# Batch norm over 64 tiles: the stores of the first 61 tiles move from ScalarE's hardware queue to GpSimd's software queue

## The chip, the cores and the metric

The kernel runs on one core of one Trainium2 chip. The metric is the device time of one execution in microseconds (us); lower is better. The profiles come from the hardware profiler, one execution each.

## The reference

Batch normalisation with given statistics, in float32, on an input of 32 x 256 x 128 x 128. Mean, variance, gamma and beta have one value per channel (256 of them).

```python
return gamma * (x - mean) / np.sqrt(var + eps) + beta
```

Per channel this is one multiplication and one addition per element. The input is 536.9 MB and so is the output.

## The kernel before

The input is seen as 64 tiles of 128 channels by 16384 values: 128 partitions with 64 KB each, 8.39 MB a tile. Three buffers in SBUF hold one tile each; tile i uses buffer i % 3 and is normalised in place. A short beginning loads the four parameter vectors and turns them into `scale_t` and `shift_t`, one column per half of the channels.

The order of the work is written out by hand, engine by engine, with semaphores (`loaded`, `stored` per buffer, `vdone` and `adone` for the two compute engines).

- **Loads** are issued by SyncE (SP). Tile 0 comes in two halves (L90, L97). Tiles 1 and 2 follow at once (L104). From tile 3 on, a load waits first until its buffer's store has landed (L103) and then until VectorE has done the first part of the tile before it. So one load is in flight at a time.
- **VectorE (DVE)** waits until a tile has landed and does its first 14336 columns in two instructions: columns 0 to 2560 (`STEP`), then 2560 to `VCOLS` (L132). The first of the two releases the next load.
- **ScalarE (ACT)** does the last 2048 columns (L143). In the loop it waits for both VectorE parts of the tile and for the landing of the store before, then computes, and then issues the tile's store (L156):

```python
for i in range(last):
    nc.scalar.wait_ge(vdone, 2 * (i + 1))
    inst = scalar_part(i, VCOLS)
    if i:
        inst._wait_ge(stored[(i - 1) % NBUF], 16 * ((i - 1) // NBUF + 1))
    store(i)
```

So one store is in flight at a time too, except at the end: the last tile is split at column 9216 (`VLAST`) between the two engines, ScalarE computes its share on landing, and the last store doesn't wait for the one before.

GpSimd (POOL) does nothing in the loop. At the end SP waits for the three `stored` semaphores (L174).

Of the kernel before, what the change touches and what calls it, by code (L numbers as in the profile page):

```python
# [6 lines left out]


NBUF = 3
PAD = 936  # L10


STEP = 2560
VCOLS = 14336
VLAST = 9216


@with_exitstack
def kernel(
    ctx: ExitStack,  # L20
    tc: tile.TileContext,
    x: bass.AP,
    gamma: bass.AP,
    beta: bass.AP,
    running_mean: bass.AP,
    running_var: bass.AP,
    out: bass.AP,
):
    nc = tc.nc
    eps = 1e-5  # L30
    f32 = mybir.dt.float32

    N, C, H, W = x.shape
    P = nc.NUM_PARTITIONS
    assert C % P == 0
    NCB = C // P
    HW = H * W
    NT = N * NCB
    B = 32
    NQ = P // B  # L40
    NE = 16
    NPAR = 4

    xr = x.rearrange("n (cb p) h w -> (n cb) p (h w)", p=P)
    outr = out.rearrange("n (cb p) h w -> (n cb) p (h w)", p=P)

    params = ctx.enter_context(tc.tile_pool(name="params", bufs=1))
    data = ctx.enter_context(tc.tile_pool(name="data", bufs=1))
    params.tile([P, PAD], f32, name="pad", tag="pad")
    bufs = [data.tile([P, HW], f32, name=f"t{s}", tag=f"t{s}") for s in range(NBUF)]  # L50
    rows = params.tile([B, NPAR * C], f32, name="rows", tag="rows")
    turned = params.tile([B, NPAR * C], f32, name="turned", tag="turned")
    par = params.tile([P, NPAR, NCB], f32, name="par", tag="par")
    eps_t = params.tile([P, 1], f32, name="eps_t", tag="eps")
    std_t = params.tile([P, NCB], f32, name="std_t", tag="std")
    rstd_t = params.tile([P, NCB], f32, name="rstd_t", tag="rstd")
    scale_t = params.tile([P, NCB], f32, name="scale_t", tag="scale")
    ms_t = params.tile([P, NCB], f32, name="ms_t", tag="ms")
    shift_t = params.tile([P, NCB], f32, name="shift_t", tag="shift")

    loaded = [tc.alloc_semaphore(f"loaded{s}") for s in range(NBUF)]
    stored = [tc.alloc_semaphore(f"stored{s}") for s in range(NBUF)]
    early = tc.alloc_semaphore("early")
    vdone = tc.alloc_semaphore("vdone")
    adone = tc.alloc_semaphore("adone")
    fetched = tc.alloc_semaphore("fetched")
    vec = tc.alloc_semaphore("vec")
    act = tc.alloc_semaphore("act")  # L70

    with tc.tile_critical():  # L72
        count = [0]

        def step(inst, sem=None, value=None):

            if sem is not None:
                inst._wait_ge(sem, value)
            elif count[0]:
                inst._wait_ge(vec, count[0])  # L80
            inst.then_inc(vec, 1)
            count[0] += 1
            return count[0]

        left, right = slice(0, HW // 2), slice(HW // 2, HW)
        last = NT - 1

        nc.sync.dma_start(out=bufs[0][:, left], in_=xr[0][:, left]).then_inc(early, 16)  # L90
        zeroed = step(nc.vector.memset(rows[:], 0.0))  # L91
        for r, ap in enumerate((running_var, gamma, beta, running_mean)):
            inst = nc.sync.dma_start(out=rows[0:NE, r * C : (r + 1) * C], in_=ap.partition_broadcast(NE))  # L93
            if r == 0:
                inst._wait_ge(vec, zeroed)
            inst.then_inc(fetched, 16)
        nc.sync.dma_start(out=bufs[0][:, right], in_=xr[0][:, right]).then_inc(loaded[0], 16)  # L97
        for i in range(1, NT):
            s, turn = i % NBUF, i // NBUF


            if turn:
                nc.sync.wait_ge(stored[s], 16 * turn)  # L103
            inst = nc.sync.dma_start(out=bufs[s][:], in_=xr[i]).then_inc(loaded[s], 16)  # L104
            if turn:
                inst._wait_ge(vdone, 2 * (i - 1) + 1)


        step(nc.vector.memset(eps_t[:], eps))  # L109
        step(nc.vector.transpose(out=turned[:], in_=rows[:]), fetched, 16 * NPAR)  # L110

        blocks = turned.rearrange("p (rc q b) -> p rc q b", q=NQ, b=B)
        flat = par.rearrange("p r cb -> p (r cb)")
        for q in range(NQ):
            placed = step(nc.vector.tensor_copy(out=flat[q * B : (q + 1) * B], in_=blocks[:, :, q, 0]))  # L115
        var_t, gamma_t, beta_t, mean_t = (par[:, r] for r in range(NPAR))
        nc.scalar.activation(  # L117
            out=std_t[:],
            in_=var_t,
            func=mybir.ActivationFunctionType.Sqrt,  # L120
            bias=eps_t[:],
            scale=1.0,
        )._wait_ge(vec, placed).then_inc(act, 1)
        step(nc.vector.reciprocal(out=rstd_t[:], in_=std_t[:]), act, 1)  # L124
        step(nc.vector.tensor_mul(out=scale_t[:], in0=gamma_t, in1=rstd_t[:]))  # L125
        step(nc.vector.tensor_mul(out=ms_t[:], in0=mean_t, in1=scale_t[:]))  # L126
        ready = step(nc.vector.tensor_sub(out=shift_t[:], in0=beta_t, in1=ms_t[:]))  # L127
        nc.vector.wait_ge(vec, ready)

        def vector_part(i, first, end):  # L130
            t, cb = bufs[i % NBUF], i % NCB
            return nc.vector.tensor_scalar(  # L132
                out=t[:, first:end],
                in0=t[:, first:end],
                scalar1=scale_t[:, cb : cb + 1],
                scalar2=shift_t[:, cb : cb + 1],
                op0=mybir.AluOpType.mult,
                op1=mybir.AluOpType.add,
            ).then_inc(vdone, 1)

        def scalar_part(i, first):
            t, cb = bufs[i % NBUF], i % NCB
            return nc.scalar.activation(  # L143
                out=t[:, first:],
                in_=t[:, first:],
                func=mybir.ActivationFunctionType.Identity,
                bias=shift_t[:, cb : cb + 1],
                scale=scale_t[:, cb : cb + 1],
            ).then_inc(adone, 1)

        def landed(i):
            return loaded[i % NBUF], 16 * (i // NBUF + 1)

        def store(i):
            s = i % NBUF
            nc.scalar.dma_start(out=outr[i], in_=bufs[s][:])._wait_ge(adone, i + 1).then_inc(stored[s], 16)  # L156

        vector_part(0, 0, HW // 2)._wait_ge(early, 16)
        vector_part(0, HW // 2, VCOLS)._wait_ge(*landed(0))
        for i in range(1, NT):  # L160
            vector_part(i, 0, STEP)._wait_ge(*landed(i))
            vector_part(i, STEP, VLAST if i == last else VCOLS)
        for i in range(last):
            nc.scalar.wait_ge(vdone, 2 * (i + 1))
            inst = scalar_part(i, VCOLS)
            if i:
                inst._wait_ge(stored[(i - 1) % NBUF], 16 * ((i - 1) // NBUF + 1))
            store(i)
        scalar_part(last, VLAST)._wait_ge(*landed(last))
        nc.scalar.wait_ge(vdone, 2 * NT)  # L170
        store(last)

        for s in range(NBUF):
            nc.sync.wait_ge(stored[s], 16 * ((NT - s + NBUF - 1) // NBUF))  # L174


# [28 lines left out]
```

## Time and profile before

| | |
|---|---|
| median of 3 runs | 2483.6 us (2483.05 to 2484.41) |
| span of the profiled execution | 2481.0 us |
| what lies around the span, by the runs' median | 2.6 us |
| busy: DVE, ACT, POOL | 508.8, 139.8, 0.2 us |
| DMA | 1073.85 MB, mean 433 GB/s over the span |
| issue to landing, median: load of a tile, store of a tile | 37.0 us, 36.5 us |

The span goes from the first to the last instruction that the profiler recorded. The profiled execution has no separate time of its own: its span is set against the runs' median. The DMA share is the mean busy share of the core's 16 DMA engines. Queue q1 carries SyncE's loads and q10 ScalarE's stores; a packet of either is a partition's row of 64 KB. Issuing a DMA is not counted as an engine's busy time.

### The profile page before, as it was taken

To read this page: it belongs to the slowest core of one execution; us is meant where nothing else is said; L and a number is where in the kernel's file an instruction comes from. 1 tells how busy PE (TensorE), PEld (TensorE's weight loads), DVE (VectorE), ACT (ScalarE), POOL (GpSimd) and SP (SyncE) were. 2 spreads that over 40 slices of the span, in tenths; PEclk is the share of its full clock that TensorE was granted. 3 is DMA by queue.
4 is the path that set the end of the run, shared out by engine and by line. 5 is a ranking of instruction groups with operands and counts; after the bars stand their busy time and mean duration, and the time that the engine had idled before them with its cause. 6 is when DMAs were issued, how large, how long until landed. Compare 5 with 4: busy or idle time off the path is not lost.

```text
span 2481.0 us, 516 instructions
## 1 busy us (share of the span) xinstructions
DVE 508.8 (21%) x139; ACT 139.8 (6%) x66; POOL 0.2 (0%) x4
## 2 busy tenths in 40 slices
DVE  2122121221212212122121221212212122121120
ACT  0000000000000000000000000000000000000001
POOL 0000000000000000000000000000000000000000
DMA  9999999999999999999999999999999999999999
GB/s 411 435 440 428 433 440 432 430 440 432 430 440 437 427 438 436 428 437 436 432 433 438 430 434 437 432 432 437 434 431 436 437 428 437 437 428 435 437 432 402
DMA packets 18708, 1073.85 MB, mean 433 GB/s; under 512 B 2128, under 2 KB 2192, under 8 KB 2192
## 3 DMA queue, kind: packets, MB, share of 16 engines
q1 hardware_dynamic: 9488, 536.94, 50.0%
q10 hardware_dynamic: 9216, 536.88, 49.9%
q14 instruction: 4, 0.03, 0.0%
HBM read 536.94 MB, written 536.87 MB: 433 GB/s over the span
## 4 chain that ended last, share of the span: by engine, by line
DMA 92%; DVE 4%; another core or an unknown queue 2%; ACT 0%; issue 0%; SPq 0%; DVEq 0%
DMA t<-in_x_dram 92%; DVE t L132 4%; ACT t L143 0%; SPq L93 0%; DVE rows L91 0%; DVE eps_t L109 0%; DVEq L200 0%; SPq L72 0%
## 5 line engine op out<-in xcount | busy, mean ns | idle before, releaser
L132 DVE TENSOR_SCALAR t<-t,scale_t,shift_t 128x11776 f32<-128x11776 f32 (+2 forms) x128 | 505.3, 3989 | 1928.8 <-DMA t<-in_x_dram 1928.7
L143 ACT ACTIVATE t<-t,shift_t,scale_t 128x2048 f32<-128x2048 f32 x64 | 138.2, 2159 | 2297.8 <-DMA out_dram<-t 2274.9
L110 DVE STREAM_TRANSPOSE turned<-rows 32x1024 f32<-32x1024 f32 x1 | 1.2, 1232 | 11.8 <-DMA rows<-in_running_mean_dram 11.8
L117 ACT ACT_TABLE_LOAD x1 | 1.3, 1283 | 0.9 <-SPq L72 0.9
L91 DVE MEMSET rows<- 32x1024 f32 x1 | 0.9, 912 | 1.2 <-SPq L72 1.2
L117 ACT ACTIVATE std_t<-par,eps_t 128x2 f32<-128x2 f32 x1 | 0.3, 295 | 14.0 <-DVE par L115 14.0
L115 DVE COPY par<-turned 32x8 f32<-32x8 f32 x4 | 0.6, 162 | 0.1
L124 DVE RECIPROCAL rstd_t<-std_t 128x2 f32<-128x2 f32 x1 | 0.2, 166 | 0.4 <-ACT std_t L117 0.4
L125 DVE TENSOR_TENSOR scale_t<-par,rstd_t 128x2 f32<-128x2 f32 x1 | 0.2, 162 | 0.0
L127 DVE TENSOR_TENSOR shift_t<-par,ms_t 128x2 f32<-128x2 f32 x1 | 0.2, 162 | 0.0
L126 DVE TENSOR_TENSOR ms_t<-par,scale_t 128x2 f32<-128x2 f32 x1 | 0.2, 160 | 0.0
L189 POOL MEMSET const-bfloat16-1.0<- 128x1 bf16 x1 | 0.1, 101 | 0.0
L189 POOL MEMSET const-uint8-127<- 128x1 uint8 x1 | 0.1, 101 | 0.0
L189 POOL MEMSET const-float32-0.0<- 128x1 f32 x1 | 0.1, 98 | 0.2 <-issue 0.2
L189 POOL MEMSET const-float32-1.0<- 128x1 f32 x1 | 0.1, 98 | 0.0
L109 DVE MEMSET eps_t<- 128x1 f32 x1 | 0.1, 59 | 0.1
## 6 DMA issues: line engine op xcount, KB each, us to landing
t<-in_x_dram SPq DMA_DIRECT2D x2, 4096.0 KB, 15.9
out_dram<-t ACTq DMA_DIRECT2D x64, 36.5
t<-in_x_dram SPq DMA_DIRECT2D x63, 37.0
rows<-in_running_var_dram SPq DMA_DIRECT2D x1, 16.0 KB, 11.1
rows<-in_gamma_dram SPq DMA_DIRECT2D x1, 16.0 KB, 10.9
rows<-in_beta_dram SPq DMA_DIRECT2D x1, 16.0 KB, 10.7
rows<-in_running_mean_dram SPq DMA_DIRECT2D x1, 16.0 KB, 10.6
```

The costliest lines, as they stand in the source:

```text
L91: zeroed = step(nc.vector.memset(rows[:], 0.0))
L109: step(nc.vector.memset(eps_t[:], eps))
L110: step(nc.vector.transpose(out=turned[:], in_=rows[:]), fetched, 16 * NPAR)
L115: placed = step(nc.vector.tensor_copy(out=flat[q * B : (q + 1) * B], in_=blocks[:, :, q, 0]))
L117: nc.scalar.activation(out=std_t[:], in_=var_t, func=mybir.ActivationFunctionType.Sqrt, bias=eps_t[:], scale=1.0,)._wait_ge(vec, placed).t ...
L124: step(nc.vector.reciprocal(out=rstd_t[:], in_=std_t[:]), act, 1)
L125: step(nc.vector.tensor_mul(out=scale_t[:], in0=gamma_t, in1=rstd_t[:]))
L126: step(nc.vector.tensor_mul(out=ms_t[:], in0=mean_t, in1=scale_t[:]))
L127: ready = step(nc.vector.tensor_sub(out=shift_t[:], in0=beta_t, in1=ms_t[:]))
L132: return nc.vector.tensor_scalar(out=t[:, first:end], in0=t[:, first:end], scalar1=scale_t[:, cb : cb + 1], scalar2=shift_t[:, cb : cb + 1 ...
L143: return nc.scalar.activation(out=t[:, first:], in_=t[:, first:], func=mybir.ActivationFunctionType.Identity, bias=shift_t[:, cb : cb + 1] ...
L189: nc = _bacc.Bacc("TRN2", target_bir_lowering=False, num_devices=1)
```

## The change

The stores of tiles 0 to 60 are issued by GpSimd, on its software queue, with `single_packet=True`. Each waits for the landing of the store before, for both VectorE parts and for ScalarE's part of its tile. The last three stores (`NTAIL`) stay on ScalarE's hardware queue and count on semaphores of their own (`closed`); of them, those of tiles 61 and 62 wait for the landing of the store before. ScalarE now waits for a tile's landing alone before it computes, in all tiles. When the store of tile 60 has landed, GpSimd executes a DRAIN. SP waits for six semaphores at the end. Loads, VectorE's work, the buffers and the split of the columns are the same.

```diff
+NTAIL = 3
...
+    closed = [tc.alloc_semaphore(f"closed{s}") for s in range(NBUF)]
...
+        soft = NT - NTAIL
+
+        def written(i):
+            if i < soft:
+                return stored[i % NBUF], 16 * (i // NBUF + 1)
+            return closed[i % NBUF], 16
+
         def store(i):
             s = i % NBUF
-            nc.scalar.dma_start(out=outr[i], in_=bufs[s][:])._wait_ge(adone, i + 1).then_inc(stored[s], 16)
+            if i < soft:
+                if i:
+                    nc.gpsimd.wait_ge(*written(i - 1))
+                nc.gpsimd.wait_ge(vdone, 2 * (i + 1))
+                inst = nc.gpsimd.dma_start(out=outr[i], in_=bufs[s][:], single_packet=True)
+            else:
+                nc.scalar.wait_ge(vdone, 2 * (i + 1))
+                if i < last:
+                    nc.scalar.wait_ge(*written(i - 1))
+                inst = nc.scalar.dma_start(out=outr[i], in_=bufs[s][:])
+            inst._wait_ge(adone, i + 1).then_inc(written(i)[0], 16)
...
-        for i in range(last):
-            nc.scalar.wait_ge(vdone, 2 * (i + 1))
-            inst = scalar_part(i, VCOLS)
-            if i:
-                inst._wait_ge(stored[(i - 1) % NBUF], 16 * ((i - 1) // NBUF + 1))
-            store(i)
-        scalar_part(last, VLAST)._wait_ge(*landed(last))
-        nc.scalar.wait_ge(vdone, 2 * NT)
-        store(last)
+        nc.scalar.wait_ge(vec, ready)
+        for i in range(NT):
+            scalar_part(i, VLAST if i == last else VCOLS)._wait_ge(*landed(i))
+            store(i)
+
+        nc.gpsimd.wait_ge(*written(soft - 1))
+        nc.gpsimd.drain()
 
         for s in range(NBUF):
-            nc.sync.wait_ge(stored[s], 16 * ((NT - s + NBUF - 1) // NBUF))
+            nc.sync.wait_ge(stored[s], 16 * ((soft - s + NBUF - 1) // NBUF))
+            nc.sync.wait_ge(closed[s], 16)
```

## The prediction, made before the changed kernel ran

> **What bounds the kernel now.** I read the page first (busy shares, DMA queues), then the windows by stage, the chain of waits in order of time, the DMA view in short stretches, and the groups by shape.
>
> From the page, the span and who is busy; in the queue lines, packets, MB and share of the 16 engines' span:
>
> ```profile
> span 2481.0 us, 516 instructions
> ...
> DMA  9999999999999999999999999999999999999999
> ...
> q1 hardware_dynamic: 9488, 536.94, 50.0%
> q10 hardware_dynamic: 9216, 536.88, 49.9%
> ```
>
> q1 carries the loads, q10 the stores. Together they fill 99.9% of the DMA engines; DVE has 21%, ScalarE 6%. The windows (start:end, length, DVE, ACT and POOL busy, clock, DMA share, GB/s) say where the missing part is:
>
> ```profile
> 0.00:62.00 62.00, 17.95 (x15) 3.67 (x3) 0.20 (x4) 1.00 0.97 408
> 62.00:2418.00 2356.00, 485.57 (x123) 127.64 (x61) 0.00 (x0) 1.00 1.00 434
> 2418.00:2481.00 63.00, 5.27 (x2) 8.46 (x2) 0.00 (x0) 1.00 0.93 403
> ```
>
> Only the first and last stretch are short of 434 GB/s: 3% of 62 us and 7% of 63 us, about 6 us in all. The 62 tiles between run with no idle DMA time. Nothing that only moves compute can bring a gain there; what can change the time is the DMA going idle. The chain of one tile (start, length, what) shows how near that is:
>
> ```profile
> 978.96 36.96 DMA t<-in_x_dram
> 1015.92 0.03 issue
> 1015.95 1.62 DVE t L132
> 1017.57 0.02 issue
> 1017.59 36.98 DMA t<-in_x_dram
> ```
>
> Only one load is in flight at a time: a load lands, DVE does its first 2560 columns, and only then is the next load issued. For these 1.67 us, and the start-up after them, there is no load. The DMA view of 2.4 us stretches around this landing (1016.8, 1024.0 and 1026.4 us) shows what fills the hole (queue: packets, MB, share):
>
> ```profile
> DMA packets 16, 1.05 MB, mean 437 GB/s; under 512 B 0, under 2 KB 0, under 8 KB 0
> q10 hardware_dynamic: 16, 1.05, 100.8%
> ...
> q10 hardware_dynamic: 10, 0.66, 63.0%
> q1 hardware_dynamic: 6, 0.39, 37.8%
> ...
> q1 hardware_dynamic: 10, 0.66, 63.0%
> q10 hardware_dynamic: 6, 0.39, 37.8%
> ```
>
> In the hole every engine moves store packets only. When both queues have work, the shares swap each 2.4 us: 10 engines on a store and 6 on a load, then the reverse. So each engine takes one 64 KB packet from one queue, then one from the other. A 8.39 MB transfer is 128 such packets, 8 per engine; a period of 38.64 us (1017.59 less 978.96) is 16 turns of 2.414 us. This taking of turns is what spreads a store over 36.5 us, so that one is always there when a load lands.
>
> **The change, part by part.** The durations of compute come from the groups by shape:
>
> ```profile
> L132 DVE TENSOR_SCALAR t<-t,scale_t,shift_t 128x11776 f32<-128x11776 f32 x62 | 397.3, 6407 | 0.0
> L143 ACT ACTIVATE t<-t,shift_t,scale_t 128x2048 f32<-128x2048 f32 x63 | 131.8, 2092 | 2285.3 <-DMA out_dram<-t 2274.9 <-DVE t L132 10.5
> L132 DVE TENSOR_SCALAR t<-t,scale_t,shift_t 128x2560 f32<-128x2560 f32 x63 | 101.6, 1613 | 1927.1 <-DMA t<-in_x_dram 1927.1
> ```
>
> *ScalarE on landing.* Its 2.09 us run beside DVE's 1.61 + 6.41 = 8.02 us instead of after the previous store's landing. The store of a tile can be issued 8.02 us after the tile lands. Alone this would take 2.1 us out of the gap between two stores; loads fill that gap now, so it is worth nothing at the end.
>
> *61 issues move from ScalarE to GpSimd.* On GpSimd each store waits for the store before it, DVE and ScalarE; only the next store is queued behind. SP's queue keeps its instructions and waits. No row shows a store issued by GpSimd. The nearest rows are SP's first load (issued at 0.95 us, packets from about 2.0, so 1.0 us to the first packet) and, far off, 8.02 us if GpSimd had to wait for a whole DVE tile. I take 2 us, between a hardware start and DVE's work but nearer the start; the ends 1.0 and 8.0 stay for the range. The Trainium skill (DMA: Bandwidth & Descriptors, Specifications) gives about 1 us to the first byte on this path against 0.6, an estimate of 0.4 us more than hardware; no run here shows it, and by it the start would be 1.4 us. In the forecast the start lies beside a running load and costs nothing.
>
> *One packet per store.* The diff sets `single_packet=True`. If the engine's turn is a packet, as the swapping shares show, a store's turn becomes 8 x 2.414 = 19.3 us on every engine, with no load packet in between. The Trainium skill (DMA: Bandwidth & Descriptors, Queues, rings and completion order) says the same as a rule: an engine "drains a whole packet (≈9-17 descriptors typical, spec ceiling ≤64) from one row's ring before switching"; the trace agrees for single 64 KB packets (2.414 us a turn), and nothing in it has a longer one.
>
> Follow a tile that lands at T with no store in flight. At T+1.67 the next load is issued, at T+2.7 its packets begin. At T+8.0 the store is issued, at T+10 its packet is there; the load has finished 3 packets and is in the 4th, so the burst runs from about T+12.4 to T+31.7. Four load packets remain: 9.7 us, to T+41.4, and the load is seen to land near T+42. The store finished 10 us before, and the next cannot be issued before T+50. So when that load lands nothing is in flight, and the cycle repeats. The same follows from any start: a burst and its wait for one turn take about 22 us plus the start, while a load needs at least 38.6, so stores always run out of tiles.
>
> The DMA is then idle from the last load packet to the first packet of the next load: about 0.4 us until DVE sees the landing (my estimate: the span ends 1.8 us after the last store packet, final barrier included), 1.67 us for DVE's first part and the issue, 1.0 us to the first packet, and 0.8 us because the landing counts the last of 16 engines (their first packets spread over about that much). 3.87 us a tile. It occurs at the landings of tiles 2 to 60, 59 times: 228 us. Bounds: 2.7 us without wake-up and spread (159 us), 5.0 us with twice of both (295 us).
>
> *Last three stores on ScalarE's queue.* These take turns of 64 KB again; the tail is as before, a few us either way. *Semaphores and DRAIN.* The DRAIN sits behind store 60's landing, more than two tiles (80 us) before the end, with nothing behind it on GpSimd; SP waits for six semaphores instead of three after everything has landed. Zero; at the end of the program, uncovered, well under the 1.8 us that the tail has now.
>
> *Sum.* Span 2481.0 + 228 = 2709 us. The runs' median lies 2.6 us above the profiled span, so 2712 us.
>
> **The rivals.**
>
> *Stores still take turns by 64 KB (the flag does not lengthen a turn), and the phase holds.* The store's gap is then 2 us instead of 2.09 + 0.34 + about 0.7 = 3.1 us from landing to first packet. A change of less than a turn leaves the alternation as it is. For: the period stood still at 16 turns all through the run although the two gaps differ. Against: the flag is in the program. Time: 2484 us, 2480 to 2491 with a turn lost at the start or end.
>
> *Turns of 64 KB, but the phase slips.* Now a store lands 24.1 us after a load (1015.95 to 1040.06 in the timeline), 16 us away from either limit: the tile not yet computed, or the buffer not yet free for the next load. If GpSimd starts over about half a turn later than hardware did (beyond 4.3 us from landing), or over half a turn earlier (below 1.5), each period gains or loses a turn, and after about seven tiles both queues wait on the same event. Then 1 to 3 us a tile are idle: 59 x 1 to 59 x 3, 2540 to 2660 us. A slip that settles sooner costs only 5 to 15 us. The Trainium skill (SBUF — State Buffer, the "DVE blocks DMA" trap) says that GpSimd cannot write descriptors during DVE's two-port operations; stores released in DVE's 8 us would start that much later, the slip's condition. No run here shows such a wait.
>
> *Faster: fewer packets, less overhead.* 448 packet boundaries per engine fewer. Were each worth 12 ns, 5 us would go: 2478 us. Against: consecutive packets start 2.414 us apart whichever queue came before, 27.1 GB/s per engine, and no gap between records is seen. The stretches outside full rate hold only 6 us, which the change leaves alone.
>
> **How the numbers follow.** The burst 0.50 (its own range 2640 to 2780); turns kept and phase held 0.25, of which nearly all within 0.2% (5 us, about what a measurement of this kernel can tell from no change); phase slipped 0.19, all but a little of it slower; faster 0.06. Slower: 0.50 + 0.18 + 0.02 = 0.70; same 0.24; faster 0.06. The likeliest case gives 2712. The range must reach down to the held phase to leave out less than 2 in 10, and up to the burst's upper bound: 2480 to 2775.
>
> **What would show it.** Right: stores landing in about 22 us after issue instead of 36.5, loads in about 40; stretches of 2.4 us with no q1 packets for 19 us in a row; a DMA share near 0.91 in the middle windows; a period near 42.5 us. Wrong: two queues still swapping each 2.4 us and a period of 38.64 us (held phase), or that swapping with idle slices (slip). A GpSimd issue that waits for DVE's end would show in the timeline as a store starting just behind DVE's second part.

## The result, and the profile after

The changed kernel takes 2580.1 us (median of 5 runs, 2571.2 to 2582.3) against 2483.6 us before: ratio 1.0381, 95% interval 1.0367 to 1.0395. It is slower by 3.8%, in the forecast range and in the forecast direction, but by 96 us instead of 228. The profiled execution took 2575.6 us, with a span of 2573.8.

The page after; q0 is the software queue. Columns of the queue lines: packets, MB, share of 16 engines' span.

```profile
span 2573.8 us, 524 instructions
...
q1 hardware_dynamic: 9488, 536.94, 51.2%
q0 software_dynamic: 8784, 511.71, 45.9%
q10 hardware_dynamic: 432, 25.17, 2.3%
...
t<-in_x_dram SPq DMA_DIRECT2D x63, 38.9
out_dram<-t POOLq DMA_DIRECT2D x61, 37.1
```

Two things to see. A store still takes 37 us from issue to landing, so it still shares the engines with a load: there is no burst of 19 us. And the added time sits in the load's queue. The times of the packet records, added up and divided by the 16 engines, give 1317 us for q1 against 1241 before (+76) and 1239 us for the stores in both kernels. What the packets leave of the span grows from 1 to 18 us (+17). Together that is the 93 us that the span gained: partly idle engines, mostly load packets that take longer than 2.418 us. The shares on the page, times the span, say the same within their rounding.

The windows by stage put it into the middle of the run:

```profile
0.00:62.00 62.00, 16.50 (x15) 5.76 (x4) 0.87 (x5) 1.00 0.99 407
62.00:2510.00 2448.00, 483.04 (x123) 127.77 (x61) 31.98 (x60) 1.00 1.00 418
2510.00:2574.00 64.00, 9.27 (x3) 6.36 (x1) 0.00 (x0) 1.00 0.90 380
```

GpSimd's 0.53 us for each issue are counted as its busy time here, unlike the issues of SyncE and ScalarE. There are 418 GB/s where there were 434. A busy share of 1.00 hides it, because a longer packet counts as busy: here the GB/s column is the one to read. The chain of one tile:

```profile
977.70 39.43 DMA t<-in_x_dram
1017.13 0.03 issue
1017.16 1.62 DVE t L134
1018.78 0.02 issue
1018.80 36.50 DMA t<-in_x_dram
```

The steps between landing and next issue are the same as before. The loads of this stretch take 36.4 to 39.6 us instead of a steady 36.96 to 36.98. And the waits say on what a store waits (the first line is of the kernel before, the other two of the changed one):

```profile
ACT t L143 <- DMA out_dram<-t: 2274.9, 62, 43.4
...
POOL out_dram L170 <- DVE t L134: 1696.2, 43, 41.1
POOL out_dram L170 <- DMA out_dram<-t: 704.0, 18, 42.8
```

Of 61 stores, 43 wait for compute of their own tile, 18 for the store before. In the kernel before, all but the first and the last store were held by the one before. The stores have moved ahead in time against the loads, up to the limit that compute sets. Where a store's landing lies behind a load's is called the phase here. VectorE starts with a load's landing, and an instruction released by a store starts 0.03 us (ScalarE) or 0.5 us (GpSimd) after that store's landing, so the timelines show the phase. First two lines of the kernel before:

```profile
1015.95 7.94 DVE L132 TENSOR_SCALAR t<-t,scale_t,shift_t 128x2560 f32<-128x2560 f32 x2 [30.69 <-DMA t<-in_x_dram]
...
1040.06 2.09 ACT L143 ACTIVATE t<-t,shift_t,scale_t 128x2048 f32<-128x2048 f32 x1 [36.51 <-DMA out_dram<-t]
```

Then the first tiles of the changed kernel:

```profile
93.33 7.93 DVE L134 TENSOR_SCALAR t<-t,scale_t,shift_t 128x2560 f32<-128x2560 f32 x2 [28.37 <-DMA t<-in_x_dram]
...
108.47 0.53 POOL L170 DMA_DIRECT2D out_dram<-t  x1 [35.89 <-DMA out_dram<-t]
...
134.88 7.93 DVE L134 TENSOR_SCALAR t<-t,scale_t,shift_t 128x2560 f32<-128x2560 f32 x2 [33.61 <-DMA t<-in_x_dram]
145.58 0.53 POOL L170 DMA_DIRECT2D out_dram<-t  x1 [36.57 <-DMA out_dram<-t]
...
176.75 7.94 DVE L134 TENSOR_SCALAR t<-t,scale_t,shift_t 128x2560 f32<-128x2560 f32 x2 [33.94 <-DMA t<-in_x_dram]
185.27 0.53 POOL L170 DMA_DIRECT2D out_dram<-t  x1 [39.16 <-DVE t L134]
```

A store used to land 24.1 us after a load. By the landings on record this falls here to 14.6, 10.2 and 4.8 us within the first tiles; from tile 4 on most stores wait for VectorE, and the phase stays near 4.8 (most tiles) or 9.7.

The DMA view in stretches of 2.4 us around the landing at 1017.13 us shows the consequence (stretches from 1016.8, 1024.0, 1026.4, 1028.8, 1031.2 and 1033.6 us):

```profile
DMA packets 16, 0.98 MB, mean 410 GB/s; under 512 B 1, under 2 KB 1, under 8 KB 1
q0 software_dynamic: 16, 0.98, 94.5%
...
q1 hardware_dynamic: 16, 1.05, 101.1%
...
q1 hardware_dynamic: 16, 1.05, 142.9%
...
DMA packets 2, 0.13 MB, mean 55 GB/s; under 512 B 0, under 2 KB 0, under 8 KB 0
...
q0 software_dynamic: 15, 0.98, 94.5%
q1 hardware_dynamic: 1, 0.07, 6.3%
...
q1 hardware_dynamic: 15, 0.98, 94.4%
q0 software_dynamic: 1, 0.07, 6.3%
```

The store is at its last packets when the load lands. Then the load is alone for four packets (the store of the tile cannot be issued before 1025.68). The fourth of these packets, just before the store's packets begin, is long: 16 packets start that hold 142.9% of the stretch, and in the next stretch only two packets start. Afterwards the engines move in step, 15 on one queue and 1 on the other, where before they were 10 and 6. On average (tiles 4 to 61) the first packets of a load take 2.81 us, the fourth 3.17, and the others 2.42 to 2.47. So of the 93 us about 23 sit in the first packets, 45 in the fourth, 17 in idle engines and the rest in the other packets.

### The profile page after: what moved, and what is told of

It is laid out like the page before. It is cut to its first block, busy times and chain, and to the rows that moved or that the text cites. A ratio compares the mean times of both kernels' runs of the same rounds, so it can differ in the third digit from the quotient of the medians.

```text
span 2573.8 us, 524 instructions
## 1 busy us (share of the span) xinstructions
DVE 508.8 (20%) x139; ACT 139.9 (5%) x66; POOL 32.8 (1%) x65
## 4 chain that ended last, share of the span: by engine, by line
DMA 92%; DVE 4%; another core or an unknown queue 2%; ACT 0%; issue 0%; SPq 0%; DVEq 0%
DMA t<-in_x_dram 92%; DVE t L134 4%; ACT t L145 0%; SPq L95 0%; DVE rows L93 0%; DVE eps_t L111 0%; DVEq L219 0%; SPq L74 0%
## 5 line engine op out<-in xcount | busy, mean ns | idle before, releaser
L170 POOL DMA_DIRECT2D out_dram<-t x61 | 32.6, 535 | 2400.2 <-DVE t L134 1696.2
```

Source lines behind the costliest of these rows:

```text
L170: inst = nc.gpsimd.dma_start(out=outr[i], in_=bufs[s][:], single_packet=True)
```

## The experiments

Theory P (phase): what counts is the length of two gaps, the load's (landing to the first packet of the next load) and the store's (likewise). If they match, the taking of turns holds its phase; if the store's is shorter by half a turn or more, stores slip early up to the compute limit and the hole at the landing is no longer covered. Theory Q: the software queue itself makes load packets slow.

By the records the store's gap is 5.5 to 7.0 us in the kernel before, in the first tiles 6.0 to 6.4, against 6.1 to 6.4 for the load. In the first tiles of the changed kernel it is 4.2 to 4.5 us against 6.3. These are counted to the first of the 16 engines' packets. The expectations below give the store's gap up to half a us longer. Each ratio is against the kernel before.

### e1: the hardware queue, ScalarE on landing

```diff
-            if i < soft:
-                ...
-                inst = nc.gpsimd.dma_start(out=outr[i], in_=bufs[s][:], single_packet=True)
+            nc.scalar.wait_ge(vdone, 2 * (i + 1))
+            if 0 < i < last:
+                nc.scalar.wait_ge(*written(i - 1))
+            inst = nc.scalar.dma_start(out=outr[i], in_=bufs[s][:])
...
-        nc.gpsimd.wait_ge(*written(soft - 1))
-        nc.gpsimd.drain()
```

> All 64 stores stay on ScalarE's hardware queue, ScalarE computes on landing; no software queue, no DRAIN. Theory P (phase: the store's gap from landing to first packet became shorter, 4.5 to 4.8 us instead of 6.0 to 7.2, so each store moves ahead until it waits for compute, and the hole at each load's landing is no longer covered): the gap is again about 2.1 us shorter than before, the store lands about 5 us after a load instead of 24.1 us, and the time is near 2575 us (2540 to 2600). Theory Q (the software queue itself slows load packets, 75 us of longer q1 packets in the trace): the time is 2484 us.

2600.9 us, ratio 1.0463 (1.0446 to 1.0481), just above the range expected. The timeline (start, us, engine, line):

```profile
1027.12 7.93 DVE L134 TENSOR_SCALAR t<-t,scale_t,shift_t 128x2560 f32<-128x2560 f32 x2 [32.76 <-DMA t<-in_x_dram]
1028.76 41.91 SPq L106 DMA_DIRECT2D t<-in_x_dram  x2
1035.13 0.34 ACTq L169 DMA_DIRECT2D out_dram<-t  x1
```

The store is issued when VectorE is done (1027.12 + 7.93), not when the store before lands. By the packet records the store's gap is 3.5 to 3.8 us in the first tiles, against 5.5 to 6.0 for the load; stores then slip to 4.8 us behind the load's landing and stay there in nearly all tiles, where in the changed kernel a quarter stand near 9.7. Q falls: there is no software queue here, and the kernel is slower still. Why it is slower still is not shown.

### e2: the software queue, ScalarE held

```diff
-            scalar_part(i, VLAST if i == last else VCOLS)._wait_ge(*landed(i))
+            if 0 < i < soft:
+                nc.scalar.wait_ge(*landed(i))
+                inst = scalar_part(i, VCOLS)
+                inst._wait_ge(*written(i - 1))
+            else:
+                scalar_part(i, VLAST if i == last else VCOLS)._wait_ge(*landed(i))
```

> The changed kernel with one wait restored: ScalarE's part of tiles 1 to 60 waits for the landing of the store before, so 2.1 us of compute lie again between a store's landing and the next store. Stores stay on the software queue. Theory P: the gap is 6.6 to 6.9 us as before, stores land about 24 us after loads, and the time is 2484 us (2480 to 2495). Theory Q: 2530 us if only the load packet next to a store's start stays long (0.76 us times 61), 2575 us if all of it stays.

2485.2 us, ratio 1.0008 (0.9999 to 1.0017): one wait gives back all of it. Its page and its timeline:

```profile
span 2485.6 us, 584 instructions
...
q1 hardware_dynamic: 9488, 536.94, 50.1%
q0 software_dynamic: 8784, 511.71, 47.5%
```

```profile
1019.85 7.94 DVE L134 TENSOR_SCALAR t<-t,scale_t,shift_t 128x2560 f32<-128x2560 f32 x2 [30.73 <-DMA t<-in_x_dram]
...
1039.16 2.09 ACT L145 ACTIVATE t<-t,shift_t,scale_t 128x2048 f32<-128x2048 f32 x1 [36.55 <-DMA out_dram<-t]
1041.54 0.53 POOL L170 DMA_DIRECT2D out_dram<-t  x1 [38.11 <-ACT t L145]
```

A store lands 19.3 us after the load (1039.16 less 1019.85), in the middle of the load that follows, and does so in every tile from 4 to 60 within 0.7 us; P had expected 24 us. The load packets are back at 50.1% of the span. The store's gap is 6.0 to 6.9 us, the load's 5.2 to 6.5. The software queue costs nothing that can be measured here.

### e3 and e4: without the flag, without the DRAIN

```diff
-                inst = nc.gpsimd.dma_start(out=outr[i], in_=bufs[s][:], single_packet=True)
+                inst = nc.gpsimd.dma_start(out=outr[i], in_=bufs[s][:])
```

> The changed kernel without the flag for one packet per store. If the flag lengthens no turn (the trace of the changed kernel has 64 KB turns), the time stays at 2575 to 2582 us, and both P and Q expect that. If the flag did matter in another way, the time moves by more than 10 us.

```diff
-        nc.gpsimd.drain()
```

> The changed kernel without the DRAIN on GpSimd. P and Q: no change beyond the spread of the changed kernel (2571 to 2582 us). A third theory, that the DRAIN costs something at the end, would give several us less.

2582.8 us, ratio 1.0398 (1.0375 to 1.0421), and 2579.5 us, ratio 1.0386 (1.0365 to 1.0407). Both intervals overlap that of the changed kernel. Neither the flag nor the DRAIN moves the time.

### e5 and e11: a shorter gap of the loads

```diff
-STEP = 2560
+STEP = 512      # e5; 1024 in e11
```

> The changed kernel with STEP = 512: VectorE's first part is about 1.1 us shorter, so the next load is issued about 1.1 us sooner after a landing; everything else as in the changed kernel. Theory P (stores run early, up to the compute limit, and the hole between the last store packets and the first packets of the next load is uncovered): the hole shrinks by about 1.1 us a tile, the time falls by up to 60 us, to 2515 to 2555 us. A rival (R: the loss comes from where the first store packets meet the load, the load's fourth packet being the longest) expects no change: 2570 to 2585 us.

> The changed kernel with STEP = 1024: the load's gap is about 0.8 us shorter than with 2560, 0.3 us longer than in e5. Theory P: load gap 5.1 to 5.8 us against a store gap of 4.5 to 5, still within a turn, so the phase holds in most executions: 2484 to 2520 us. If the match has to be closer than about half a us, stores slip early again: 2540 to 2570 us.

e5: 2489.7 us, ratio 1.0022 (1.0011 to 1.0032), nearly all of the loss gone, more than the 60 us expected. So the hole doesn't merely shrink. R, which expected no change, doesn't account for the loss by itself; the long fourth packet that it names is real all the same. The ratio is that of nine executions, which took 2483 to 2496 us; the profiled one took 2550.8 us, and it alone has a trace. In its first tiles the load's gap is 4.5 us, as long as the store's 4.5, and the phase is no longer lost to the early side. But the stores drift late, in steps to 31 us behind a load and by the middle of the run to about 38. That the phase holds in the nine others is concluded from their time alone.

e11: 2506.1 us, ratio 1.0099 (1.0084 to 1.0115), within the expected 2484 to 2520; but the store's landing wanders between 4.8 and 21.9 us behind the load's. For tiles 31 to 45 it stands at 21.7 us, with gaps of 4.2 to 4.6 us on both sides; elsewhere the two differ by up to 1.4 us, less than a turn, and the phase moves.

### e6b and e12: slower compute

```diff
+VLATE = 4096    # e6b; 2624 in e12
...
-            vector_part(i, STEP, VLAST if i == last else VCOLS)
+            vector_part(i, STEP, VLAST if i == last else VLATE)
...
-            scalar_part(i, VLAST if i == last else VCOLS)._wait_ge(*landed(i))
+            scalar_part(i, VLAST if i == last else VLATE if i else VCOLS)._wait_ge(*landed(i))
```

> The changed kernel, but from tile 1 on ScalarE does columns 4096 to 16384 on landing (12288 columns, about 10.6 us by the two sizes in the profile) and VectorE is done after about 3 us: a tile is ready for its store about 10.6 us after landing instead of 8.0, so compute is slower. Theory P: at the early limit the store is held back by 2.6 us, about one turn of 2.414 us, so it ends later past the next load's landing and covers more of the hole; the time falls below the changed kernel's 2580 us, to 2484 to 2550 us. A rival (compute on the path of store and load costs what it takes) expects 60 x 2.6 = 156 us more: about 2735 us.

> The kernel of e6b with the split at column 2624: ScalarE does 13760 columns, about 11.9 us by the sizes in the profile, 1.1 to 1.3 us more than in e6b. Theory P: the store is held about half a turn longer; where e6b's stores landed 9.7 us after a load (four turns), these land about 12.1 us after (five turns), the rest of e6b's 23 us goes, and the time is 2484 to 2496 us. If e6b's rest has nothing to do with where the store lands, it stays at 2506 us; if longer compute costs, 2506 + 60 x 1.2 = 2578 us.

A first form, e6, with the split at 4096 in every tile, has no time: it leaves VectorE an empty part in tile 0.

e6b: ScalarE's part takes 10.63 us, a tile is ready 2.6 us later than in the changed kernel, and the time falls by 74 us to 2506.0 (ratio 1.0092, 1.0077 to 1.0108). Stores now wait for ScalarE:

```profile
POOL out_dram L171 <- ACT t L146: 2191.4, 57, 39.3
```

They land 9.7 us behind a load, one more pair of turns. By the records the idle time falls from 18 to 2 us and the excess of load packets from 76 to 22. The compute limit is where the stores stand, and a later limit covers the hole. e12 is a miss: with 11.85 us the store still lands 9.7 us behind the load, and the time is 2504.6 us (1.0074 to 1.0107). The rest of some 20 us did not go. It sits mostly in the load's last packets before the store's begin (2.5 to 2.65 us on average instead of 2.418); P does not explain those.

### e7: the kernel before with a short ScalarE part

```diff
-VCOLS = 14336
+VCOLS = 16128
```

> The kernel before with VCOLS = 16128: ScalarE's part, which lies between a store's landing and the next store, shrinks from 2.09 to about 0.6 us, and VectorE's grows by about 1 us. Hardware queue, every wait as before. Theory P: the store's gap falls from 6.0-7.2 to about 4.5-5.7 us from landing to first packet, stores slip early until compute holds them, and the time is 2530 to 2600 us. If the loss needs anything of the change itself (queue, ScalarE on landing), it stays at 2483 us.

2562.6 us, ratio 1.0319 (1.0304 to 1.0335). No wait and no queue was changed, only the split: ScalarE's part, which is the store's delay, is 1.5 us shorter, and VectorE's 0.9 us longer. The store's gap is 4.1 to 4.5 us in the first tiles, against 6.0 for the load, and stores slip early as in the changed kernel. Half of them then wait for their own tile's compute:

```profile
ACT t L143 <- DVE t L132: 1294.2, 33, 41.0
ACT t L143 <- DMA out_dram<-t: 1151.8, 30, 44.1
```

Longer compute is no cost by itself (e6b). So the loss needs nothing of the change but the shorter gap.

### e8 and e9: the other side

```diff
-VCOLS = 14336
+VCOLS = 11264   # in the kernel of e2
```

> The kernel of e2 (software queue, ScalarE's part behind the store before) with VCOLS = 11264: ScalarE's part grows to about 4.65 us, so the store's gap grows from 6.7 to about 9.3 us, a whole turn more. Theory P, its other side: stores now fall behind by up to a turn a tile until a load has to wait for its buffer; 2540 to 2660 us. If only starting too early is harmful, 2485 us.

```diff
             inst = nc.sync.dma_start(out=bufs[s][:], in_=xr[i]).then_inc(loaded[s], 16)
-            if turn:
-                inst._wait_ge(vdone, 2 * (i - 1) + 1)
```

> The changed kernel with the loads' wait for VectorE's first part taken out: a load waits only until its buffer's store has landed. The load's gap is gone while buffers are free. Theory P in its wider form (the gaps of loads and stores have to match within a turn): the loads now run ahead until each has to wait for a store's landing, where both queues start together, as in e8; 2550 to 2740 us. Rival (only the hole after a load's landing costs, so no gate means no hole): 2484 us.

e8: 2736.6 us, ratio 1.1016 (1.0997 to 1.1034); e9: 2728.7 us, ratio 1.0986 (1.0971 to 1.1001). In both the loads run ahead until each waits for its buffer. The DMA queue's own waits of e8 and e9:

```profile
SPq L105 <- DMA out_dram<-t: 2589.4, 61, 66.7
...
SPq L106 <- DVE t L134: 27.7, 4, 13.7
```

```profile
SPq L106 <- DMA out_dram<-t: 2608.6, 61, 64.4
```

All 61 loads wait for a store's landing, and the next store is released by the same landing, so nothing covers the start of either. About 4 us a tile: dearer than I expected for e8 (2540 to 2660), and as expected for e9. A ScalarE part 2.6 us too long is worse than one 2.1 us too short, and taking out the loads' gate, with no gap left at all, is just as bad.

In e9 something else comes in: GpSimd's issue of a store falls into VectorE's work on another tile, and lasts until 0.1 us after the end of that work. With VectorE idle it takes 0.53 us.

```profile
335.24 7.94 DVE L132 TENSOR_SCALAR t<-t,scale_t,shift_t 128x2560 f32<-128x2560 f32 x2 [36.83 <-DMA t<-in_x_dram]
...
338.45 4.84 POOL L168 DMA_DIRECT2D out_dram<-t  x1 [39.92 <-DMA out_dram<-t]
```

The same holds for the stores of tiles 5 to 60, whose first packets come about 9.5 and 6.9 us by turns after the start of the issue; in e8 they come after 5.0. How much of e9's loss this makes is not shown; e8 has it in one store alone and loses as much.

### e10: loads alone

The stores of tiles 0 to 60 are left out, with the waits for them.

```diff
-                nc.sync.wait_ge(stored[s], 16 * turn)
+                nc.sync.wait_ge(adone, i - NBUF + 1)
...
-            store(i)
+            if i >= soft:
+                store(i)
...
```

> The changed kernel without the stores of tiles 0 to 60 (left out, so most of the output is not written; a load waits for ScalarE instead of the store). It prices an uncovered load gap by itself: 8 packets of 2.414 us, then about 3.0 us to the first packet of the next load and the spread of 16 engines. 22.7 to 23.5 us a tile, 1450 to 1510 us in all. If load packets are long (2.8 us first, more than 3 us later) also here, the longer packets are the load's own start after an idle engine; if all but the first take 2.418 us, the long fourth packet of the changed kernel needs a store that begins.

1555.1 us, a single execution; above the expected total, because the start and the last three tiles with their stores add to some 60 periods. The period itself is as expected:

```profile
697.99 21.79 DMA t<-in_x_dram
719.79 0.03 issue
719.81 1.62 DVE t L134
721.44 0.02 issue
721.45 21.79 DMA t<-in_x_dram
```

A period is 23.46 us, 8 turns of 2.414 us are 19.31: an uncovered gap costs 4.15 us a tile. By the packet records the first packet of each load takes 3.09 us on average, all others 2.42 to 2.44. So the long first packet is the load's own start on idle engines. The long fourth packet of the changed kernel is not there without the stores. In e8 it is the third packet that is long, 3.51 us on average, again the last before the store's first.

## Why the prediction was right or wrong

- **What bounds the kernel** held: all that was lost is lost at the DMA engines, and e6b shows that compute may grow by 2.6 us a tile with a gain.
- **One packet per store** was the step that failed. I took the flag to make a turn of 8 x 2.414 us. The stores take turns of 64 KB as before, 37 us from issue to landing with the flag and without it (e3). The burst that carried half the chance, the store of 22 us and the 228 us do not exist; 96 us were lost, to another cause. That the kernel came out slower, as forecast, is luck as far as the burst goes. The Trainium skill's rule (DMA: Bandwidth & Descriptors, Queues, rings and completion order), that an engine finishes a packet before it changes queues, agrees with the trace for single 64 KB packets; that the flag joins a store's eight into one was my addition, and the trace shows otherwise.
- **ScalarE on landing, "worth nothing at the end"** was the second failed step. I named the work that covers the store's gap but not what the gap does: it keeps stores and loads apart. Taking it away alone costs 4.6% (e1); putting it back takes the whole loss away (e2).
- **The held phase** failed on its margin: I let a gap change of less than a turn pass. It also mis-sized the gaps: I took 3.1 us against 2, a change of 1.1. The store's gap was 6.0 to 6.4 us in the first tiles and fell to 4.2 to 4.5, by about 2 us, which is between half a turn and a turn, and the phase was lost in three tiles. What the 3.1 us lacked is a wait at busy engines: the store issued at 1042.18 us had its first packet 3.5 us later, where I had 1.0.
- **The phase slips** is what happened, at the early limit, and its 2540 to 2660 us holds the 2580. I gave it 0.19. Its margin of half a turn fits e2, which holds, and e1, e7 and e8, which do not; e5 and e11, whose gaps are closer in most tiles and whose phase still moves, show that half a turn is no safe margin. Its price of 1 to 3 us a tile came out (93 us over some 60 tiles, 1.5 us), but partly by luck: it was meant as idle time, and only 17 of the 93 us are idle. The rest are longer load packets, which no part of the prediction had. At the late limit the price is about 4 us.
- **The price of an uncovered hole**, 3.87 us, was close: 4.15 us in e10. The changed kernel loses less because its stores still cover most of it.
- **The software queue's start**, taken as 2 us: at the compute limit a store's first packet comes on average 13.6 us after the load's landing, against 12.4 us on the hardware queue (e1), so about 1.1 us later than hardware. By the median of the 16 engines' first packets it is only 0.3 us. In the changed kernel GpSimd issued all its stores while VectorE was idle, so a wait behind VectorE's work, which the phase-slip rival counted with, played no part. There is such a wait: e9's issues last up to 5.2 us by it.
- **DRAIN**: zero, as said (e4). The tail and the semaphores were not changed by themselves; the last stretch moves 380 GB/s where it moved 403.
- **Small slips in the working**: 61 stores of 8 packets have 427 packet boundaries fewer, not 448, and half a turn below 3.1 us is 1.9, not 1.5. Neither bears on the forecast.

What stays open is why the load's last packet before a store's first is long: 3.17 us on average in the changed kernel, 2.418 us in the kernel before, where load-only stretches exist too. It holds about 45 of the 93 us. So the experiments show that the shorter gap causes the loss and where the stores then stand, but not what makes half of its price.

## What to carry to other kernels

In this kernel two DMA streams fill the engines together and each has a gap between its transfers; the time was kept only where the two gaps were nearly equal in length, to well within one packet's turn of 2.414 us. A wait that looks idle may be what keeps the streams apart. Before moving or shortening a step on such a path, ask what its length is matched to, and read GB/s and the landing of one stream against the other, tile by tile, since the busy share stays at 1.00. If a change must shorten one gap, put the delay back elsewhere (e2), or shorten the other (e5, which held less firmly).

## What was not expected of the hardware

Engines read as busy while they lose time: 76 of 93 us are longer load packets, up to 4.5 us for 64 KB that otherwise take 2.418 us. A load that starts on idle engines pays 0.67 us in its first packet (e10). And the phase between the two streams mostly stands at whole turns: the offsets between landings that recur in the traces, 24.1, 19.3, 14.5, 9.7 and 4.8 us, are multiples of 2.414 us. The kernel before holds one of them to 0.1 us from tile 6 to tile 60, and the changed kernel loses it in three.
